# The delta rule's decay in the copy of the values, and its state products as two of 64 rows

## The chip, the cores and the metric

The kernel runs on one core of one Trainium2 chip. The metric is the device time of one execution in microseconds; lower is better.

## What is computed

Two transformer blocks stand one behind the other. The first has a token mixer and a mixture of 32 experts; the second has two layers of attention and feed-forward on 256 + 16 tokens. The change touches only the mixer's gated delta rule, which runs for 8 heads of width 128, forward and backward over 256 context tokens and then 256 latent tokens, in chunks of 64. Cut to what matters:

```python
kd = k * jnp.exp(g[..., -1:] - g)[..., None]      # decay from each token to its chunk's end
gl = jnp.exp(g[..., -1])
...
def step(s, xs_n):                                # one chunk; s is the 128 x 128 state of a head
    u_n, w_n, attn_n, qg_n, kd_n, gl_n = xs_n
    v_new = u_n - jnp.einsum('bhck,bhkv->bhcv', w_n, s)
    o_n = jnp.einsum('bhck,bhkv->bhcv', qg_n, s) + jnp.einsum('bhij,bhjv->bhiv', attn_n, v_new)
    s = s * gl_n[..., None, None] + jnp.einsum('bhck,bhcv->bhkv', kd_n, v_new)
    return s, o_n
```

The sum over a chunk's 64 tokens of `kd` times `v_new` is the same whether the decay, one number for each token, multiplies the key or the value.

## The kernel before

One program holds the mixer and the experts' weights of the first block, and the second block behind them. In the mixer, the projections of the input by `w_in` are float32 products in three parts each (`mm3`, L164): ACT rounds a weight piece to its high part (L150), DVE takes the low part (L151), and PE runs high·high, high·low and low·high. A framework schedules each engine's instructions: it takes the program as written and reorders it by what is ready in its own reckoning, so the order on an engine isn't the order of the code. Memory and PSUM tiles come from pools with a fixed number of buffers for each tag.

The delta rule runs in an order written as a string of letters (`DELTA_ORDER`, L169): K, Q and V are the convolved projections, M and X a group's inverse matrices, H is `head_setup` for one head, S is `scan_step` for a pair of heads, and small letters are fill work, mainly projections of other parts of the mixer. There are four pairs of heads, each with two H and eight S, one after the other.

`head_setup` (L649) copies the keys to token-major form (`kt`, by `to_tok`, L647), builds the attention matrix `A2` (L666, L667) and the inverse `TT` (L677 to L688; `Dt`, `Dn`, `Z`, `E` in the trace). Then it makes two arrays of 8 steps x 128 columns, by four instructions of 64 partitions x 512 elements each (L695): `vs`, the values times beta, on DVE, and `ks`, the keys times the decay `eDL`, on POOL. `comb` (L455 on) puts forward chunk `cf` into one half of the partitions of step n and backward chunk `cb` into the other. POOL also clears `vb` (L702), a 128 x 256 tile for each of two steps in turn.

`scan_step` (L706) treats both directions of one head at once. For step n:

- `p1` (L718, L719): two products of the state `st` with the keys, 64 output rows each, in two column halves of the array, which run side by side. DVE makes `r` from it (L721).
- `vn` (L724): TT times `r`, 128 x 128.
- ACT copies `vn`'s forward rows into columns 0 to 127 of `vb` (L726) and its backward rows into columns 128 to 255 (L727); the rest of `vb` stays zero.
- in steps 4 to 7 the outputs `o1` (L731, L732), a second copy of `vn` (L734), `o2` (L736), and their sum (L737, L738).
- `pu` (L742): one product of `ks` with `vb`, 128 x 128 weights and 256 columns, which gives both directions' state update thanks to the zeros. In step 0 DVE copies it to `st` (L744), later it adds it to the decayed state, 128 columns at a time (L746, L748). Step 7 has none, so there are 56 such products.

At a pair's end DVE adds the two directions' outputs (L756). PSUM's eight banks go to `mm` (2), `sm` (2), `ch` (3, the small products above) and `pu` (1). Behind the delta rule, four heads of gated linear attention (GLA) use `pu` for two products each (L866, L870). Tiles `y` are the mixer's 12 large buffers (three for each pair: `TT`, `vs`, `ks`), of which three are alive at a time.

Behind the mixer the experts' weights are loaded by the SP queue as buffers come free and multiplied as they arrive.

Of the kernel before, what the change touches and what calls it, by code (L numbers as in the profile page):

```python
# [9 lines left out]
F32 = mybir.dt.float32  # L10
F32R = mybir.dt.float32r
I32 = mybir.dt.int32
AF = mybir.ActivationFunctionType
# [180 lines left out]
def phase1(k, A, B):  # L194
# [28 lines left out]
    def chps():  # L223
        return ps.tile([128, 128], F32, name=k.nm("ch"), tag="ch", bufs=3)
# [5 lines left out]
    def big(shape, dt=F32):  # L230

        return y8.tile([128] + shape, dt, name=k.nm("y8"), tag="y8")
# [227 lines left out]
    ceG = one.tile([128, 8, 8], F32, name="ceG")  # L460
    comb(cnbe, lambda r, d, q: nc.vector.tensor_copy(d, tv(nbe[:, :, 8 * q:8 * q + 8])[r]))
    comb(ceG, lambda r, d, q: nc.vector.tensor_copy(d, tv(eG[:, :, 8 * q:8 * q + 8])[r]))

# [80 lines left out]
    def fill_mod(j):  # L544
        mp = ps.tile([128, 512], F32, name=k.nm("ch"), tag="ch", bufs=3)
# [104 lines left out]
    def head_setup(h, TT, vs, ks):  # L650
# [48 lines left out]
        comb(ks, scaled(nc.gpsimd, kt, eDL))  # L699
        st = wd.tile([128, 256], F32, name=k.nm("st"), tag="st", bufs=2)  # L700
        vb = wd.tile([128, 2, 256], F32, name=k.nm("vb"), tag="vb", bufs=2)
        nc.gpsimd.memset(vb, 0.0)  # L702
        os_ = wd.tile([128, 4, 128], F32, name=k.nm("os"), tag="os", bufs=2)
        return A2, TT, vs, ks, st, vb, os_

    def scan_step(p, n):  # L706
# [5 lines left out]
        for h in hs:  # L712
            A2, TT, vs, ks, st, vb, os_ = sets[h]
# [11 lines left out]
            vq = vb[:, u]  # L725
            nc.scalar.copy(vq[rf, 0:128], vn[rf])  # L726
            nc.scalar.copy(vq[rb, 128:256], vn[rb])  # L727
# [12 lines left out]
            if n < 7:  # L740
                pu = ps.tile([128, 256], F32, name=k.nm("pu"), tag="pu", bufs=1)
                nc.tensor.matmul(pu, ks[:, n, :], vq, start=True, stop=True)  # L742
                if n == 0:
                    nc.vector.tensor_copy(st, pu)  # L744
                else:
                    nc.vector.scalar_tensor_tensor(st[:, 0:128], st[:, 0:128], gl[:, h, cf:cf + 1],  # L746
                                                   pu[:, 0:128], op0=ALU.mult, op1=ALU.add)
                    nc.vector.scalar_tensor_tensor(st[:, 128:256], st[:, 128:256], gl[:, 8 + h, cb:cb + 1],  # L748
                                                   pu[:, 128:256], op0=ALU.mult, op1=ALU.add)
# [11 lines left out]
    for c in DELTA_ORDER:  # L761
# [25 lines left out]
        elif c == "H":  # L787
            if i % 2 == 0:
                trio = [big([2, 8, 128]) for _ in range(3)]
            sets[i] = head_setup(i, *(x[:, i % 2] for x in trio))  # L790
# [769 lines left out]
T2 = 272  # L1560
# [539 lines left out]
```

## Time and profile before

| | us |
|---|---|
| median of 3 runs (lowest, highest) | 2473.36 (2466.64, 2479.65) |
| the profiled execution, its own time | 2471.81 |
| span of its instructions | 2470.0 |
| PE busy in the span | 2284.5 (92%) |
| DVE busy | 1243.4 (50%) |
| ACT busy | 925.4 (37%) |
| POOL busy | 151.0 (6%) |

The delta rule's scans and setups lie between 165 and 480 us of the span, GLA and the merge behind them to about 690, the experts to about 1700, and the second block behind those. The 1.8 us between the span and the execution's own time lie before and after the recorded instructions. An engine's share over the whole span mixes these stages, so the rows are read by stretches: in each one, which engine is busy for nearly all of it, and what the others wait for. In a timeline, a row is one instruction or a run of like ones (x count); the time in brackets is idle time of that engine just ahead of it, with the instruction that ended it. A float32 product shows as two passes (x2) on PE.

### The profile page before, as it was taken

How to read it: one execution, taken by the hardware profiler on the slowest of the kernel's cores; microseconds unless marked ns; L12 is line 12 of the kernel's file. 1: busy time of each engine (PE TensorE's matmuls, PEld its weight loads, DVE VectorE, ACT ScalarE, POOL GpSimd, SP SyncE). 2: the span in 40 equal slices, each digit the busy share in tenths (PEclk: the TensorE clock that was granted, in tenths of full speed). 3: DMA queues.
4: the chain of work that ended last, by engine and by line, in shares of the span. 5: the costliest groups of instructions: out<-in, count | busy, mean ns of one | idle time of the engine just before them, and what ended most of it. 6: DMA issues, size and time to landing. Idle time of an engine off the chain costs nothing.

```text
span 2470.0 us, 36281 instructions
## 1 busy us (share of the span) xinstructions
PE 2284.5 (92%) x14402; PEld 1546.0 (63%) x14403; DVE 1243.4 (50%) x2676; ACT 925.4 (37%) x1956; POOL 151.0 (6%) x186
## 2 busy tenths in 40 slices
PE   6789978999989999999899999998999999999998
PEld 3466646889983333333334333334877999887998
DVE  4898897587561111112211111114867556866655
ACT  4556546577441101010101010103475545465544
POOL 0122012000010000000000000000011001011001
PEclk8889988999999999999999999999999999999999
DMA  8522431134898999999999999996524555534563
GB/s 286 142 77 52 120 120 35 45 94 121 254 329 325 416 416 416 416 416 416 388 415 415 416 415 416 416 416 237 157 84 151 179 175 160 153 103 140 188 187 104
DMA packets 290347, 605.87 MB, mean 245 GB/s; under 512 B 26038, under 2 KB 218681, under 8 KB 254332
## 3 DMA queue, kind: packets, MB, share of 16 engines
q1 hardware_dynamic: 283236, 595.24, 65.8%
q10 hardware_dynamic: 6280, 7.80, 1.2%
q8 instruction: 115, 1.88, 0.3%
q14 instruction: 60, 0.49, 0.1%
q0 software_dynamic: 656, 0.46, 0.1%
HBM read 602.30 MB, written 1.15 MB: 244 GB/s over the span
## 4 chain that ended last, share of the span: by engine, by line
PE 35%; DMA 9%; DVE 4%; issue 2%; ACT 1%; POOL 0%; ACTq 0%; SPq 0%; DVEq 0%; POOLq 0%
PE qm L164 23%; DMA w<-in_w_gu_dram 6%; PE yd L1374 2%; DMA w<-in_w_down_dram 2%; PE gt L1358 2%; PE lt L1358 2%; PE qm L1811 1%; DVE wl L151 1%; PE tr L1343 1%; DVE u L1617 0%; PE tr L1287 0%; PE qp L1878 0%; ACT wh L150 0%; PE lt L1363 0%; PE qp L1823 0%
## 5 line engine op out<-in xcount | busy, mean ns | idle before, releaser
L150 ACT CAST wh<-w 128x1024 fp32r<-128x1024 f32 (+2 forms) x318 | 318.4, 1002 | 284.7 <-PE qm L164 203.0
L151 DVE TENSOR_TENSOR wl<-w,wh 128x1024 fp32r<-128x1024 f32 (+2 forms) x318 | 371.1, 1168 | 40.5 <-ACT wh L150 38.9
L1253 ACT ACTIVATE sg<-g 128x1024 f32<-128x1024 f32 x16 | 16.9, 1057 | 727.3 <-DVE g L1251 682.7
L164 PE MATMUL qm<-uh,wh 128*128 128x272 f32 (+2 forms) x1008 | 261.4, 293 | 0.5 <-ACT wh L150 0.3
L164 PE MATMUL qm<-ul,wh 128*128 128x272 f32 (+2 forms) x1008 | 258.0, 289 | 1.0 <-DVE ul L151 1.0
L1251 DVE TENSOR_SCALAR g<-gt 128x1024 f32<-128x1024 f32 x16 | 19.6, 1225 | 469.4 <-PE gt L1363 413.9
L1374 PE MATMUL yd<-w,aT 128*64 128x512 f32 x1024 | 228.4, 600 | 0.2 <-ACT aT L1265 0.2
L164 PEld LDWEIGHTS qm<-uh,wh 128*128 128x128 f32 (+1 forms) x1008 | 188.9, 188 | 10.2 <-issue 5.8
L164 PEld LDWEIGHTS qm<-ul,wh 128*128 128x128 f32 (+1 forms) x1008 | 189.7, 188 | 2.9 <-DVE ul L151 1.4
L1358 PE MATMUL lt<-w,resB 128*64 128x512 f32 x512 | 189.5, 594 | 0.6 <-DVE act L1252 0.6
L1358 PE MATMUL lt<-w,xg 128*64 128x512 f32 x512 | 188.4, 597 | 0.0
L1358 PE MATMUL gt<-w,resB 128*64 128x512 f32 x512 | 183.0, 600 | 5.3 <-DMA w<-in_w_gu_dram 5.3
L1358 PE MATMUL gt<-w,xg 128*64 128x512 f32 x512 | 177.3, 602 | 8.9 <-DMA w<-in_w_gu_dram 8.8
L1374 PEld LDWEIGHTS yd<-w,aT 128*64 128x64 f32 x1024 | 72.9, 138 | 143.3 <-issue 140.3
L164 PE MATMUL qm<-uh,wl 128*128 128x272 f32 (+2 forms) x1008 | 145.6, 286 | 0.0
L1273 DVE TENSOR_TENSOR ys<-yd,g2r 128x512 f32<-128x512 f32 x32 | 20.6, 686 | 248.1 <-PE yd L1374 231.4
L164 PE MATMUL mm<-hTh,wh 128*128 128x256 f32 (+1 forms) x384 | 130.6, 360 | 8.2 <-ACT wh L150 4.1
L164 PEld LDWEIGHTS qm<-uh,wl 128*128 128x128 f32 (+1 forms) x1008 | 132.7, 188 | 0.5 <-issue 0.4
L164 PE MATMUL qm<-fl,wh 128*128 128x272 f32 (+1 forms) x512 | 128.5, 286 | 0.0
L164 PE MATMUL qm<-fh,wh 128*128 128x272 f32 (+1 forms) x512 | 127.3, 286 | 0.0
L164 PE MATMUL mm<-hTl,wh 128*128 128x256 f32 (+1 forms) x384 | 126.1, 348 | 0.0
L1358 PEld LDWEIGHTS lt<-w,xg 128*64 128x64 f32 x512 | 60.4, 138 | 71.4 <-issue 69.3
(586 smaller groups left out, 4349.8 us busy)
## 6 DMA issues: line engine op xcount, KB each, us to landing
w<-in_w_gu_dram SPq DMA_DIRECT2D x256, 1024.0 KB
w<-in_w_down_dram SPq DMA_DIRECT2D x128, 1024.0 KB
w<-in_w_ff_dram SPq DMA_DIRECT2D x64, 1024.0 KB
w<-in_w_in_dram SPq DMA_DIRECT2D x72, 512.0 KB
w<-in_w_in_dram SPq DMA_DIRECT2D x30, 1024.0 KB
y<-in_w_mod_dram SPq DMA_DIRECT2D x19, 1024.0 KB
w<-in_w_out_dram SPq DMA_DIRECT2D x24, 512.0 KB
w<-in_w_mod_dram SPq DMA_DIRECT2D x5, 1024.0 KB
```

The source lines that it names most:

```text
L150: k.nc.scalar.copy(hi, x)
L151: k.nc.vector.tensor_sub(lo, x, hi.bitcast(F32))
L164: mm = nc.tensor.matmul(out, l, r, start=start and n == 1, stop=stop and n == 3 * len(terms))
L1251: nc.vector.tensor_scalar(g, gt, 7.0, LOW / 1.702, op0=ALU.min, op1=ALU.max)
L1253: nc.scalar.activation(sg, g, AF.Exp, scale=-1.702)
L1273: nc.vector.tensor_mul(ys[:, js], yd[:, js], g2r[:, js])
L1343: nc.tensor.matmul(o, hx[:, t, f * 128:(f + 1) * 128], S[t].rearrange("p e s -> p (e s)"), start=(t == 0 and i == 0), stop=(t == 1 and i = ...
L1358: nc.tensor.matmul(quarter(j)[64 * i:64 * i + 64], xg[:, kk, c0:c0 + CAP], w[i][:, j * 512:(j + 1) * 512], start=(kk == 0), stop=False)
L1374: nc.tensor.matmul(yd[64 * i:64 * i + 64, j * 512:(j + 1) * 512], aT[:, 2 * f2 + f, 64 * i:64 * i + 64], w[i][:, f, j * 512:(j + 1) * 512] ...
L1811: nc.tensor.matmul(o[r, f:], v[:n, j, r], keys(ts[i], j, n)[:, f - KQ[j]:], start=(j == 0), stop=(j == 2))
```

## The change

- The decay moves from the keys to the values. `ks` and its four POOL instructions for each head are gone, and so are `vb`'s clearing on POOL and one of three large `y` buffers for each pair. `head_setup` hands on the plain `kt` instead.
- A small table `ceDL`, the decay in step order, is built once by four small DVE copies like those of `ceG` (L462).
- One ACT instruction copies the whole `vn` (128 x 128) to `vb`, scaled by `ceDL`'s column of that step and head, in place of two copies of 64 rows. `vb` is half as wide. Step 7 has no copy any more.
- The state product is two products of 64 rows each, forward on one half of the array's rows and backward on the other: weights are 64 rows x 128 columns of `kt`, and 128 columns of values go through. Each writes a `ch` tile of its own. Step 0 copies them to `st` by two instructions of 128 columns.
- The bank of `pu` goes to `ch`, which has four buffers now. GLA's two products go to `ch` too, and its `G` moves from the tag `kt` to `vt`.

```diff
-        return ps.tile([128, 128], F32, name=k.nm("ch"), tag="ch", bufs=3)
+        return ps.tile([128, 128], F32, name=k.nm("ch"), tag="ch", bufs=4)
...
+    ceDL = one.tile([128, 8, 8], F32, name="ceDL")
...
+    comb(ceDL, lambda r, d, q: nc.vector.tensor_copy(d, tv(eDL[:, :, 8 * q:8 * q + 8])[r]))
...
         comb(vs, scaled(nc.vector, vts[hh], Bt))
-        comb(ks, scaled(nc.gpsimd, kt, eDL))
         st = wd.tile([128, 256], F32, name=k.nm("st"), tag="st", bufs=2)
-        vb = wd.tile([128, 2, 256], F32, name=k.nm("vb"), tag="vb", bufs=2)
-        nc.gpsimd.memset(vb, 0.0)
+        vb = wd.tile([128, 2, 128], F32, name=k.nm("vb"), tag="vb", bufs=2)
...
-            vq = vb[:, u]
-            nc.scalar.copy(vq[rf, 0:128], vn[rf])
-            nc.scalar.copy(vq[rb, 128:256], vn[rb])
+            if n < 7:
+                vq = vb[:, u]
+                nc.scalar.activation(vq, vn, AF.Copy, scale=ceDL[:, n, h:h + 1])
...
             if n < 7:
-                pu = ps.tile([128, 256], F32, name=k.nm("pu"), tag="pu", bufs=1)
-                nc.tensor.matmul(pu, ks[:, n, :], vq, start=True, stop=True)
-                if n == 0:
-                    nc.vector.tensor_copy(st, pu)
-                else:
-                    nc.vector.scalar_tensor_tensor(st[:, 0:128], st[:, 0:128], gl[:, h, cf:cf + 1],
-                                                   pu[:, 0:128], op0=ALU.mult, op1=ALU.add)
-                    nc.vector.scalar_tensor_tensor(st[:, 128:256], st[:, 128:256], gl[:, 8 + h, cb:cb + 1],
-                                                   pu[:, 128:256], op0=ALU.mult, op1=ALU.add)
+
+                pu = chps(), chps()
+                nc.tensor.matmul(pu[0], kt[rf, cf // 2, :], vq[rf], start=True, stop=True)
+                nc.tensor.matmul(pu[1], kt[rb, cb // 2, :], vq[rb], start=True, stop=True)
+                for d, c in enumerate((cf, cb)):
+                    sd = st[:, 128 * d:128 * d + 128]
+                    if n == 0:
+                        nc.vector.tensor_copy(sd, pu[d])
+                    else:
+                        nc.vector.scalar_tensor_tensor(sd, sd, gl[:, 8 * d + h, c:c + 1], pu[d], op0=ALU.mult, op1=ALU.add)
...
-                trio = [big([2, 8, 128]) for _ in range(3)]
-            sets[i] = head_setup(i, *(x[:, i % 2] for x in trio))
+                duo = [big([2, 8, 128]) for _ in range(2)]
+            sets[i] = head_setup(i, *(x[:, i % 2] for x in duo))
...
-        G = T2("G", "kt")
+        G = T2("G", "vt")
...
-        p0 = ps.tile([128, 256], F32, name=k.nm("pu"), tag="pu", bufs=1)
+        p0 = ps.tile([128, 256], F32, name=k.nm("pu"), tag="ch", bufs=4)
```

With the code, the scheduler's order changes through the mixer. PE in the fourth pair's early steps, before (L164 are projections that fill the time, named `tm`):

```order
L724 MATMUL ch_4138<-r_4136,y_675_3939 128x128
L164 MATMUL tm_4436<-wh_4464,hTh 128x256
L164 MATMUL tm_4436<-wh_4464,hTl 128x256
L718 MATMUL ch_4146<-st_4020,kT_2658 64x128
L164 MATMUL tm_4436<-wh_4464,hTh 128x256
L742 MATMUL pu_4142<-vb_4103,y_677_3941 128x256
L719 MATMUL ch_4146<-st_4020,kT_2658 64x128
L164 MATMUL tm_4436<-wh_4464,hTl 128x256
L164 MATMUL tm_4436<-wh_4464,hTh 128x256
```

After, the same place; L743 and L744 are the two new products, other lines of the scan keep their numbers:

```order
L724 MATMUL ch_4182<-r_4180,y_714_3947 128x128
L164 MATMUL tm_4562<-wh_4532,hTl 128x256
L164 MATMUL tm_4562<-wh_4532,hTh 128x256
L164 MATMUL tm_4562<-wh_4532,hTl 128x256
L164 MATMUL tm_4562<-wh_4532,hTh 128x256
L743 MATMUL ch_4185<-vb_4024,kt_3954 128x128
L744 MATMUL ch_4186<-vb_4024,kt_3954 128x128
L718 MATMUL ch_4191<-st_4100,kT_2726 64x128
L719 MATMUL ch_4191<-st_4100,kT_2726 64x128
L164 MATMUL tm_4562<-wh_4532,hTl 128x256
L164 MATMUL tm_4562<-wl_4533,hTh 128x256 x4
```

Before, the two halves of `p1` (L718, L719) of one head stand apart, with fill work and the other head's state product between them; in the whole scan 11 of the 56 pairs are parted so. After, all 56 pairs stand whole, nearly always right behind the two state products of the other head.

POOL from the fourth pair's setup on, before (L669 and L655 clear TT and A2; `y` from `kt` is `ks`):

```order
L669 MEMSET y_675_3939 128x1024 x2
L702 MEMSET vb_4021 128x512
L655 MEMSET A_680_3949 128x512
L702 MEMSET vb_4103 128x512
L655 MEMSET A_692_4031 128x512
L695 TENSOR_TENSOR y_677_3941<-kt_3947,tok 64x4x128
L695 TENSOR_TENSOR y_677_3941<-kt_3947,tok 64x2x2x128
L695 TENSOR_TENSOR y_677_3941<-kt_3947,tok 64x4x128
L695 TENSOR_TENSOR y_677_3941<-kt_3947,tok 64x2x2x128
```

After (the lines moved by two: L671, L657 for L669, L655; L489 clears a convolution's border, L860 is GLA's):

```order
L671 MEMSET y_714_3947 128x1024 x2
L489 MEMSET pad_3823 128x654
L489 MEMSET pad_3918 128x654
L657 MEMSET A_718_3956 128x512
L657 MEMSET A_730_4033 128x512
L860 MEMSET AT_4697 128x256
```

The eight multiplications of each pair and the clearing of `vb` are gone from POOL, 40 rows in all, and nothing else takes their place there.

On DVE the instructions stay the same but for the four copies of `ceDL` and one more copy at step 0 of each head. On SP, whose loads are ordered by free buffers, a few loads of `w_in` and `w_mod` change places. The order of the experts' work and of the second block is the same in both.

## Rows read from the trace of the kernel before

**Rows 1.** stretches: window, its length; busy us (instructions) PE, PEld, DVE, ACT, POOL; PEclk, DMA, GB/s
```profile
230.00:250.00 20.00, 18.27 (x132) 12.70 (x131) 17.61 (x32) 12.82 (x33) 10.01 (x10) 0.83 0.51 78
...
292.00:360.00 68.00, 51.59 (x430) 32.18 (x429) 63.92 (x148) 28.27 (x55) 12.13 (x15) 0.87 0.47 160
...
418.00:436.00 18.00, 12.58 (x156) 10.51 (x157) 14.73 (x22) 9.43 (x38) 11.11 (x10) 0.62 0.00 1
436.00:480.00 44.00, 44.00 (x312) 34.42 (x313) 21.70 (x60) 19.01 (x60) 0.63 (x2) 1.00 0.18 48
...
800.00:1600.00 800.00, 750.55 (x3244) 296.58 (x3242) 142.28 (x211) 73.92 (x106) 1.09 (x2) 0.99 1.01 414
```

**Rows 2.** timeline of POOL, 405 to 440: start us, us, engine, line, op, tiles, count [idle before]
```profile
420.22 10.25 POOL L695 TENSOR_TENSOR y<-kt,tok 64x512 f32<-64x512 f32 x8
```

**Rows 3.** timeline of DVE, 420 to 433
```profile
421.74 2.45 DVE L756 TENSOR_TENSOR resB<-os 64x256 f32<-64x256 f32 x2
424.20 4.35 DVE L695 TENSOR_TENSOR y<-vt,tok 64x512 f32<-64x512 f32 x3
...
429.62 3.31 DVE L695 TENSOR_TENSOR y<-vt,tok 64x512 f32<-64x512 f32 x4
```

**Rows 4.** timeline of PE, 417 to 433.5
```profile
428.70 0.77 PE L724 MATMUL ch<-y,y 128*128 128x128 f32 x2 [3.57 <-DVE y L695]
```

**Rows 5.** line L695's instructions: duration ns min/median/max, first and last start
```profile
L695 DVE TENSOR_TENSOR y<-vt,tok x32: 674/689/1536, 156.4 to 432.2; 64x512 f32<-64x512 f32 x32
L695 POOL TENSOR_TENSOR y<-kt,tok x32: 1040/1201/1500, 165.9 to 429.4; 64x512 f32<-64x512 f32 x32
```

**Rows 6.** the same view of line L756
```profile
L756 DVE TENSOR_TENSOR resB<-os x16: 406/422/1258, 228.8 to 477.9; 64x256 f32<-64x256 f32 x16
```

**Rows 7.** timeline of DVE, 227 to 247
```profile
233.95 2.84 DVE L695 TENSOR_TENSOR y<-vt,tok 64x512 f32<-64x512 f32 x3
...
237.85 4.26 DVE L695 TENSOR_TENSOR y<-vt,tok 64x512 f32<-64x512 f32 x4
```

**Rows 8.** timeline of DVE, 340 to 348
```profile
343.07 1.21 DVE L631 TENSOR_TENSOR tmp<-Ms,Ts 128x207 f32<-128x207 f32 x1
...
344.40 1.02 DVE L633 TENSOR_TENSOR Ts<-Ts,tmp 128x207 f32<-128x207 f32 x1
...
346.90 0.36 DVE L633 TENSOR_TENSOR Ts<-Ts,tmp 128x192 f32<-128x192 f32 x1
```

**Rows 9.** timeline of all engines, 445.1 to 448.4
```profile
445.53 0.59 PE L742 MATMUL pu<-vb,y 128*128 128x256 f32 x2
...
446.06 0.43 PE L719 MATMUL ch<-st,kT 128*64 128x128 f32 x2
...
446.42 0.39 PE L164 MATMUL tm<-wh,hTh 128*128 128x256 f32 x1
...
446.64 0.28 PE L164 MATMUL tm<-wh,hTl 128*128 128x256 f32 x1
...
446.76 0.29 PE L164 MATMUL tm<-wh,hTh 128*128 128x256 f32 x1
...
446.95 1.22 DVE L151 TENSOR_TENSOR wl<-w,wh 128x1024 fp32r<-128x1024 f32 x1
...
447.48 0.39 PE L724 MATMUL ch<-r,y 128*128 128x128 f32 x2
...
447.79 0.32 PE L718 MATMUL ch<-st,kT 128*64 128x128 f32 x1
...
447.95 0.26 ACT L726 COPY vb<-ch 64x128 f32<-64x128 f32 x1 [1.37 <-PE ch L724]
...
448.16 0.50 PE L164 MATMUL tm<-wl,hTh 128*128 128x256 f32 x2
```

**Rows 10.** ACT's groups, 100 to 480: line, op, shapes, count, busy us, mean ns, idle before
```profile
L727 ACT COPY vb<-ch 64x128 f32<-64x128 f32 x64 | 16.7, 260 | 0.8
```

**Rows 11.** DVE's groups, 100 to 480, the same columns
```profile
L744 DVE COPY st<-pu 128x256 f32<-128x256 f32 x8 | 3.4, 424 | 1.8 <-PE pu L742 1.7
```

More of the change, by code (lines that the diff above doesn't have):

```diff
@@ L544, in fill_mod @@
     def fill_mod(j):
-        mp = ps.tile([128, 512], F32, name=k.nm("ch"), tag="ch", bufs=3)
+        mp = ps.tile([128, 512], F32, name=k.nm("ch"), tag="ch", bufs=4)
         for kk in range(8):
@@ L648, in to_tok, with head_setup @@
         return vt
-    def head_setup(h, TT, vs, ks):
+    def head_setup(h, TT, vs):
         hh, h, (M, EA, Dn, Dt) = h, h % 4, groups[h // 4]
@@ L698, in head_setup @@
         comb(vs, scaled(nc.vector, vts[hh], Bt))
-        comb(ks, scaled(nc.gpsimd, kt, eDL))
         st = wd.tile([128, 256], F32, name=k.nm("st"), tag="st", bufs=2)
-        vb = wd.tile([128, 2, 256], F32, name=k.nm("vb"), tag="vb", bufs=2)
-        nc.gpsimd.memset(vb, 0.0)
+        vb = wd.tile([128, 2, 128], F32, name=k.nm("vb"), tag="vb", bufs=2)
         os_ = wd.tile([128, 4, 128], F32, name=k.nm("os"), tag="os", bufs=2)
-        return A2, TT, vs, ks, st, vb, os_
+        return A2, TT, vs, kt, st, vb, os_
     def scan_step(p, n):
@@ L712, in scan_step @@
         for h in hs:
-            A2, TT, vs, ks, st, vb, os_ = sets[h]
+            A2, TT, vs, kt, st, vb, os_ = sets[h]
             if n == 0:
@@ L805, in gla_gates @@
         kT, qT = gk[h], gq[h]
-        pz = ps.tile([128, 512], F32, name=k.nm("ch"), tag="ch", bufs=3)
+        pz = ps.tile([128, 512], F32, name=k.nm("ch"), tag="ch", bufs=4)
         nc.tensor.matmul(pz, gw[32 * d:32 * d + 16, h * 128:(h + 1) * 128], lr[32 * d:32 * d + 16, :], start=True, stop=True)
-        T2 = lambda nm, tag, b=2: (wd if tag == "kt" else wk).tile([128, 512], F32, name=k.nm(nm), tag=tag, bufs=b)
+        T2 = lambda nm, tag, b=2: (wd if tag == "vt" else wk).tile([128, 512], F32, name=k.nm(nm), tag=tag, bufs=b)
         z, l = T2("z", "acc"), T2("l", "e", 3)
@@ L869, in gla_gates @@
         nc.scalar.copy(ss_[:, 0, :], p0)
-        p1 = ps.tile([128, 256], F32, name=k.nm("pu"), tag="pu", bufs=1)
+        p1 = ps.tile([128, 256], F32, name=k.nm("pu"), tag="ch", bufs=4)
         nc.tensor.matmul(p1, kdt[:, 2, :], gv[h][:, 2 + fi, :], start=True, stop=True)
@@ L1040, in ev_out @@
         return fn
-    pl = [ps.tile([128, 32], F32, name=k.nm("pl"), tag="ch", bufs=3) for _ in range(2)]
+    pl = [ps.tile([128, 32], F32, name=k.nm("pl"), tag="ch", bufs=4) for _ in range(2)]
     def logits(cc):
```

## The prediction

> **What bounds the kernel now.** I read the table of stretches first [rows 1], since the shares over the whole span mix stages. While the experts run (800 to 1600), the DMA engines are busy throughout (1.01 of the window): that stage has a length of its own, and what the mixer ahead of it gains or loses shifts it by as much. So the change is worth what it moves in 165 to 480, one for one. There the limit changes from place to place. In the fourth pair's scan (436 to 480) PE is busy 44.00 of 44 us at full clock: only PE time counts. In the setups between scans PE is not full: 12.58 of 18 us at clock 0.62 in 418 to 436, 18.27 of 20 at 0.83 in 230 to 250, 51.59 of 68 at 0.87 in 292 to 360, where DVE has 63.92. These are the stretches in which POOL works (11.11 of 18 and 10.01 of 20 us). So I then read DVE and POOL there, and PE's own timeline in the scan.
>
> **POOL's products slow DVE.** L695 on DVE takes 689 ns in the median, but 1536 at worst, while the same shape on POOL takes 1201 [rows 5]. POOL's eight for the fourth pair fill 420.22 to 430.5 without a gap [rows 2], and just there three DVE ones take 4.35 us and four take 3.31, and two of L756 take 2.45 [rows 3], against 0.422 each undisturbed [rows 6]. Excess: 4.35 − 3 × 0.689 = 2.28, 3.31 − 4 × 0.689 = 0.55, 2.45 − 0.84 = 1.61, in sum 4.4. PE waits for exactly this: 3.57 us before L724, until DVE's L695 [rows 4]. After, POOL has nothing to do there. I take −6 for the place: the 4.4, and 1.6 for the clock, granted at half its speed (1.2 of 2.4 GHz) for most of the 18 us, after PE had idled; it should come back sooner. Ends: −3.6 (that wait alone) and −8.
> In the second pair the same products make three L695 take 2.84 and four take 4.26 [rows 7], excess 0.77 + 1.50 = 2.3; PE idles 1.7 of the 20 us there and is at 0.83 clock [rows 1], for which I add 1.2, so −3.5 (−1.7 to −4.2). Pair one, with as many POOL products, I price alike, a little less: −3 (0 to −4).
> For the third pair they run beside the inverse of the next group, a chain of small DVE instructions: L631 takes 1.21 and L633 1.02, and the like a little later 0.36 [rows 8], excess 0.85 + 0.66; I add 1 for the same slowing of their neighbours. DVE is the limit in that stretch, so −2.5 (0 to −3).
> Sum of this part **−15** (−5 to −19).
>
> **The state products.** Before, one keeps PE for 0.43 us: L742's first pass starts at 445.53 and the next product, L719, at 446.06, of which 0.10 go to a change of mode [rows 9]; that is 0.215 for a pass of 256 columns, 0.11 for 128. After, four passes of 128 columns and 64 rows, two on each half of the rows. No row of the mixer has that form; the nearest is L718 with L719, two halves of columns that run side by side. The whole pair, from the end of the product ahead of it (447.48 + 2 × 0.11 = 447.70) to the next fill (448.16), takes 0.46, of which 0.09 ahead (447.70 to 447.79) and as much behind are spent on getting into the other mode. Since in the new order the pair P stands right behind the state products, the step between them is shared. I take 0.42 for the two state products: 0.09 to get in, about 0.22 for the passes when the halves overlap, 0.11 for a weight load that no work hides. That is 56 × (0.42 − 0.43), about **−0.8**. Bounds: −4 if it is 0.36, as cheap as the pair without its exit; +11 if the two halves don't overlap (0.63 each, 56 × 0.2).
>
> Rows 9 show what a change of mode costs, 0.09 us each way. The Trainium skill says so as a rule (TensorEngine Tiling (Array Packing), Key Properties: a change of tiling mode, not merely of tile, drains TensorE), and it speaks against this change, which adds one more mode to each step; the trace agrees, and with the rule the state product would cost 0.1 more than before where the passes save nothing, +6 in all.
>
> **The parted pairs.** In before's order 11 of the 56 pairs P are parted. A half alone costs as much as a whole pair: from 445.96 to the next fill at 446.42 it is 0.46, and that fill is 0.22 from the next one (446.42 to 446.64) where 0.12 is usual (446.64 to 446.76) [rows 9], so 0.56 in sum. After, none is parted: 11 × 0.56 = **−6.2** (−5 to −6.5), PE time in stretches where PE is full.
>
> **What is added.** Step 0 has two copies to `st` in place of one of 424 ns [rows 11], eight times; on the way to the next step it is about +0.1 each, **+1** (0 to +2). The four copies of `ceDL` are 64 x 32 each, smaller than that, early in the mixer: **+0.7** at most, likely under DMA waits. ACT makes one copy of 128 rows in place of two of 64 rows, 260 ns each [rows 10]; with the same 128 columns I take it to last as long as one of them: each state product may start some 0.26 earlier, worth little where fills stand in between: **−1** (0 to −3).
>
> **The order.** After, the schedule is stricter: L724, four fills, the two state products and P at once, fills again. L724's result takes 0.47 to reach ACT (447.48 to 447.95) and the copy 0.26 more [rows 9]; PE gets through L724 and four fills in 0.23 + 4 × 0.12 = 0.71. So PE comes 0.02 to 0.1 early in each of 56 head-steps, and what DVE has in front of `st` and `r` adds to it now and then. The four `ch` buffers are also all used in one late step (vn, o1, o2, and two for the state), and two of GLA's products wait for them. I take **+5** (0 to +10).
>
> Sum: −15 − 0.8 − 6.2 + 1 + 0.7 − 1 + 5 = −16.3. Against the profiled execution's own 2471.81 that is 2455.5; the median of the runs is 1.5 above it, so **2457**.
>
> **Rivals.**
> - *The halves don't run side by side* (the change doesn't do what it says): two products of 64 rows cost 0.42 + 2 × 0.11, about 0.63, for each step instead of 0.43, +11, and the gains at the setups stay: 2457 + 11 = 2468. For it: both halves read `vb` and write PSUM at once, and no row shows that form; against it: L718 and L719, halves of the array too, take 0.46 with all their entering and leaving, which four passes one behind the other of 0.11 would fill by themselves.
> - *DVE or PE's place in the order takes the gain back.* POOL's products are gone, yet the setup's DVE chain keeps its length in PE's waits because new order puts other DVE work there, or fills run out at the ends of pairs two and three: half of the −15 is lost and +5 becomes +9: −16.3 + 7.5 + 4 = −5, 2468 again; range 2462 to 2474.
> - *Better*: all the DVE excess passes to the end (−19) and the state products cost 0.36 (−4): −19 − 4 − 6.2 + 1 + 2 = −26, 2447; up to 2440 where the order costs nothing.
> - *Slower*: the alternation itself. With P right behind the state products, and T's `r` behind both `st` updates on DVE, each head-step is one chain; a 1.22 us L151 [rows 9] in front of the updates then stops PE, since the fills behind it are few. To cancel 16.3 it has to cost 0.29 on top in each of the 56 head-steps, or one whole L151 in 13 of them. If it meets 24, 24 × 1.22 = +29, 2457 + 29 = 2486. For it: PE has no idle time in that stretch now, with more room between products. Against it: fills are as many as before, and the scheduler parts most L151 from the chain.
>
> **Chances.** The forecast, 2445 to 2461, has 0.53; better 0.08; the halves one behind the other 0.12; gain mostly taken back 0.17; slower 0.10, of which 0.07 lies beyond half a per cent. Half a per cent, 12.4 us, is about what a measurement of this kernel can tell from no change. The rivals at 2468 count as within it. Faster (below 2461): 0.61; same: 0.32; slower (above 2486): 0.07. The range leaves out the slower case and the best part of the better one: 2441 to 2474.
>
> **What would show it.** In the changed kernel's trace: no POOL L695; DVE's L695 all near 0.69 us, PE's wait before the fourth pair's first L724 near zero and the clock of that stretch well above 0.62 (if not, the −15 is wrong). The two state products starting 0.01 to 0.05 apart, and from the end of the fill ahead of them to P about 0.42 (0.63 would show the serial rival). No P alone. In the scans PE still near full; a wait before P or L724 on DVE of over 0.2 us in most steps would show the slower rival. The expert stage should keep its length and begin earlier by the gain; if it doesn't, a transfer sets its start, and the prediction is wrong at its first step.

## The result and the profile after

The changed kernel takes 2489.35 us (2488.23 to 2493.58, 5 runs) against 2473.36 (2466.64 to 2479.65, 5 runs) of the kernel before: 1.0065 times, with a 95% interval of 1.0046 to 1.0084. It is slower by some 16 us, where 2457 was forecast. The profiled execution took 2488.23 with a span of 2486.5.

Stretches, with the columns of [rows 1]. The bounds are the first and last L724 of a pair's scan, GLA from behind the last scan to its last state product, and from there to the first product behind the mixer, all to within 2 us (the changed kernel's bounds lie 0.9 us behind these products). First the kernel before: between the scans of pairs 1 and 2, 2 and 3, the third scan, between 3 and 4, GLA, and the mixer's rest.

```profile
228.50:236.90 8.40, 6.71 (x82) 4.70 (x80) 8.19 (x14) 7.15 (x23) 7.84 (x8) 1.00 0.00 0
292.60:367.30 74.70, 57.83 (x516) 36.66 (x514) 69.43 (x153) 33.78 (x77) 12.13 (x15) 0.89 0.47 156
367.30:417.80 50.50, 48.53 (x389) 37.56 (x385) 35.53 (x89) 32.12 (x93) 7.91 (x9) 0.97 0.19 52
417.80:428.70 10.90, 5.93 (x100) 4.47 (x100) 10.16 (x14) 7.83 (x30) 9.33 (x9) 0.66 0.01 2
474.70:596.60 121.90, 119.06 (x835) 105.09 (x834) 98.79 (x250) 87.45 (x214) 2.19 (x7) 1.00 0.32 88
596.60:660.00 63.40, 60.59 (x482) 58.87 (x480) 40.18 (x81) 41.55 (x101) 2.34 (x1) 0.97 0.72 213
```

The same six of the changed kernel:

```profile
227.50:234.00 6.50, 6.50 (x92) 4.82 (x92) 5.71 (x13) 3.66 (x9) 0.53 (x1) 1.00 0.49 164
290.30:354.00 63.70, 50.07 (x408) 34.31 (x408) 60.15 (x145) 31.96 (x70) 8.88 (x12) 0.85 0.48 163
354.00:409.90 55.90, 53.20 (x470) 41.64 (x470) 31.83 (x90) 31.98 (x89) 1.17 (x2) 0.81 0.11 30
409.90:417.10 7.20, 4.21 (x65) 3.33 (x63) 6.22 (x16) 2.99 (x13) 0.53 (x1) 0.71 0.00 0
466.00:623.00 157.00, 134.21 (x861) 114.79 (x860) 102.15 (x255) 91.59 (x221) 2.01 (x7) 0.92 0.27 76
623.00:676.70 53.70, 51.16 (x410) 49.10 (x408) 35.52 (x71) 35.77 (x88) 2.37 (x1) 1.00 0.71 211
```

The setups between scans are shorter: 8.4 to 6.5, 74.7 to 63.7, 10.9 to 7.2 us, in sum 16.6. They also hold less: counted by their start, 547 PE instructions lie in the three where before has 690, since work of the next setups moved into the scans. The first GLA product starts 10.4 us earlier (476.6 to 466.2), with 33 more of the projections' fill products (L164) already done, some 4 us. Then GLA takes 157.0 us where it took 121.9, with PE busy for 134.2 of them and a clock of 0.92 instead of 1.00: of the 35 us more, PE idles 20 (22.8 against 2.8) and is busy 15 longer, at that clock and with 38 more fill products, some 4 us. The rest of the mixer gives some 10 of that back: part of its fill work has been done by then. Counted between the starts of products: −10.4 to GLA's first, +37.2 in GLA (118.0 to 155.2), −11.0 to the first product behind the mixer (660.0 to 675.8 in the span), +0.7 in all that follows; in sum +16.5. So the loss is in one stage, and it is one that the change touches by the tags of three tiles only.

DVE's products of the values, in the view of [rows 5], and the fourth pair's setup on DVE, which answers to [rows 3]:

```profile
L697 DVE TENSOR_TENSOR y<-vt,tok x32: 673/684/691, 155.0 to 418.2; 64x512 f32<-64x512 f32 x32
```

```profile
411.55 0.85 DVE L757 TENSOR_TENSOR resB<-os 64x256 f32<-64x256 f32 x2
...
412.64 2.59 DVE L697 TENSOR_TENSOR y<-vt,tok 64x512 f32<-64x512 f32 x4
...
416.29 2.59 DVE L697 TENSOR_TENSOR y<-vt,tok 64x512 f32<-64x512 f32 x4
```

All 32 take 673 to 691 ns, where the median was 689 and the worst 1536; four of them take 2.59 us, and two of L757 (before: L756) 0.85 instead of 2.45. POOL has no instruction there.

Why GLA is longer: one direction of a head is a gate product (L807 before, L808 after), a long chain on DVE and ACT, attention products on two lines (L862 and L863 before, L863 and L864 after), three transposes, and state products on two lines (L868, L871 before; L869, L872 after). What PE waits for in GLA, by line, releaser, total us, times, longest; first before, then after:

```profile
PE ch L862 <- DVE qk L835: 2.8, 6, 0.6
```

```profile
PE ch L863 <- DVE qk L836: 15.2, 7, 5.1
```

PE's timeline at one such place, before:

```profile
486.73 0.71 PE L862 MATMUL ch<-qk 128*128 128x128 f32 x4 [0.42 <-DVE qk L835]
...
487.75 1.12 PE L807 MATMUL ch<-lr,gw 16*128 16x512 f32 x2
...
490.65 1.04 PE L868 MATMUL pu<-gv,kdt 128*128 128x256 f32 x4
...
492.23 0.65 PE L871 MATMUL pu<-gv,kdt 128*128 128x256 f32 x2
```

Attention at 486.73, the next direction's gate right behind it at 487.75, and only then, among fills, this direction's state products at 490.65 and 492.23. After, a like place:

```profile
519.06 0.71 PE L863 MATMUL ch<-qk 128*128 128x128 f32 x4 [0.15 <-DVE qk L836]
...
522.13 2.03 PE L869 MATMUL pu<-gv,kdt 128*128 128x256 f32 x4 [0.57 <-ACT kdt L858]
523.96 1.06 PE L872 MATMUL pu<-gv,kdt 128*128 128x256 f32 x2
524.95 1.44 PE L808 MATMUL ch<-lr,gw 16*128 16x512 f32 x2
...
533.45 0.77 PE L863 MATMUL ch<-qk 128*128 128x128 f32 x2 [5.14 <-DVE qk L836]
```

The gate (524.95) comes behind both state products now, 5.9 us after the attention product (519.06) instead of 1.0; over the seven handovers from one direction to the next it is 3.6 to 24.9 us instead of 1.0 to 1.5. The chain from the gate to the next attention product takes 8 to 11 us in both, where PE waits for it; started late, it outlasts the fills, and PE waits 5.14 us before L863. In all seven handovers of the changed kernel the gate stands behind L872; before, it stood ahead of L868. The granted clock falls in stretches with such waits, to 0.74 and 0.83 in these two of 20 us:

```profile
520.00:540.00 20.00, 13.43 (x44) 9.08 (x43) 13.05 (x39) 9.46 (x31) 0.31 (x1) 0.74 0.18 53
...
560.00:580.00 20.00, 15.06 (x91) 13.32 (x92) 9.89 (x25) 8.22 (x19) 0.53 (x2) 0.83 0.08 21
```

### The profile page after: what moved, and what is told of

Read it like the earlier page. It is cut to its first block, busy times and chain, and to the rows that moved or that the text cites. A ratio compares the mean times of both kernels' runs of the same rounds, so it can differ in the third digit from the quotient of the medians.

```text
span 2486.5 us, 36348 instructions
## 1 busy us (share of the span) xinstructions
PE 2288.4 (92%) x14514; PEld 1547.0 (62%) x14515; DVE 1226.2 (49%) x2688; ACT 914.3 (37%) x1884; POOL 109.7 (4%) x146
## 3 DMA queue, kind: packets, MB, share of 16 engines
q1 hardware_dynamic: 283236, 595.24, 65.6%
## 5 line engine op out<-in xcount | busy, mean ns | idle before, releaser
L151 DVE TENSOR_TENSOR wl<-w,wh 128x1024 fp32r<-128x1024 f32 (+2 forms) x318 | 373.3, 1175 | 53.8 <-ACT wh L150 52.1
L164 PE MATMUL qm<-uh,wh 128*128 128x272 f32 (+2 forms) x1008 | 261.0, 293 | 0.5 <-ACT wh L150 0.3
L164 PE MATMUL qm<-ul,wh 128*128 128x272 f32 (+2 forms) x1008 | 257.5, 289 | 0.9 <-DVE ul L151 0.9
L164 PEld LDWEIGHTS qm<-uh,wh 128*128 128x128 f32 (+1 forms) x1008 | 188.7, 188 | 10.2 <-issue 5.8
L164 PEld LDWEIGHTS qm<-ul,wh 128*128 128x128 f32 (+1 forms) x1008 | 189.4, 188 | 2.8 <-DVE ul L151 1.3
L164 PE MATMUL qm<-uh,wl 128*128 128x272 f32 (+2 forms) x1008 | 144.7, 285 | 0.0
L164 PE MATMUL mm<-hTh,wh 128*128 128x256 f32 (+1 forms) x384 | 127.1, 351 | 6.6 <-ACT wh L150 4.1
L164 PEld LDWEIGHTS qm<-uh,wl 128*128 128x128 f32 (+1 forms) x1008 | 131.9, 187 | 0.5 <-issue 0.4
L164 PE MATMUL qm<-fl,wh 128*128 128x272 f32 (+1 forms) x512 | 128.5, 286 | 0.0
L164 PE MATMUL qm<-fh,wh 128*128 128x272 f32 (+1 forms) x512 | 127.3, 286 | 0.0
L164 PE MATMUL mm<-hTl,wh 128*128 128x256 f32 (+1 forms) x384 | 123.7, 341 | 0.0
```

What stands on the lines that cost most here:

```text
L151: k.nc.vector.tensor_sub(lo, x, hi.bitcast(F32))
L164: mm = nc.tensor.matmul(out, l, r, start=start and n == 1, stop=stop and n == 3 * len(terms))
```

## The experiments

In this table "delta" is the time from the first L724 to the last, "scans" what the four scans take of it, and GLA is counted from its first gate to its last state product, all in the profiled execution; the time is the median, the ratio is to runs of the kernel before on the same chip. A profiled execution can lie up to 10 us from its kernel's median (e5_products_gla_sm 2477.76, e7_full_rows 2480.03, e8_idle_pool 2485.14). The scans don't hold the same work in all kernels, since each schedule parts setups and fill differently: 1404 PE instructions start in them before, 1690 in the changed kernel, e3, e9 and e10, 1694 in e2, 1615 in e1, 1496 in e6, 1848 in e7, 1556 in e11. Their lengths compare like with like only where these counts agree.

| kernel | us | ratio (95%) | delta | scans | GLA |
|---|---|---|---|---|---|
| before | 2473.36 | | 303.5 | 209.4 | 118.0 |
| changed | 2489.35 | 1.0065 (1.0046 to 1.0084) | 292.8 | 215.4 | 155.2 |
| e1_before_merge | 2518.17 | 1.0188 (1.0171 to 1.0205) | 325.1 | 239.7 | 153.4 |
| e2_own_bank | 2475.16 | 1.0011 (0.9996 to 1.0026) | 301.7 | 222.2 | 120.2 |
| e3_gla_sm | 2462.49 | 0.9954 (0.9941 to 0.9967) | 291.3 | 213.6 | 119.5 |
| e4_products_alone | 2493.41 | 1.0076 (1.0063 to 1.0089) | 321.4 | 217.0 | 118.3 |
| e5_products_gla_sm | 2468.72 | 0.9974 (0.9965 to 0.9983) | 303.7 | 209.1 | 121.0 |
| e6_decay_alone | 2459.73 | 0.9944 (0.9928 to 0.9961) | 286.2 | 199.6 | 121.5 |
| e7_full_rows | 2489.97 | 1.0065 (1.0050 to 1.0080) | 313.3 | 236.9 | 117.0 |
| e8_idle_pool | 2492.50 | 1.0076 (1.0062 to 1.0090) | 310.1 | 212.7 | 131.2 |
| e9_late_states | 2488.43 | 1.0064 (1.0048 to 1.0081) | 292.8 | 215.9 | 152.7 |
| e10_gates_first | 2464.82 | 0.9967 (0.9951 to 0.9982) | 290.5 | 212.3 | 120.0 |
| e11_both_heads | 2465.19 | 0.9976 (0.9959 to 0.9992) | 294.0 | 202.5 | 120.3 |

**Where the loss comes from.** The theory is that the tag `ch` is one ring of buffers whose tiles are handed out in the order of the code. GLA's state products take two of them, so the next direction's gate, which takes a `ch` tile too, can't come before them. First the merge of the banks alone, without the rest of the change:

```diff
-        return ps.tile([128, 128], F32, name=k.nm("ch"), tag="ch", bufs=3)
+        return ps.tile([128, 128], F32, name=k.nm("ch"), tag="ch", bufs=4)
...
-                pu = ps.tile([128, 256], F32, name=k.nm("pu"), tag="pu", bufs=1)
+                pu = ps.tile([128, 256], F32, name=k.nm("pu"), tag="ch", bufs=4)
...
-        p0 = ps.tile([128, 256], F32, name=k.nm("pu"), tag="pu", bufs=1)
+        p0 = ps.tile([128, 256], F32, name=k.nm("pu"), tag="ch", bufs=4)
...
```

> The kernel before with one thing of the change alone: the bank of pu goes to ch (four buffers), so that the old state product and GLA's two products take their tiles from ch in turn. Delta rule, POOL's products and the 128x256 state product stay as before. Ring theory (the loss lies in GLA, where each direction's gate tile now has to come behind the two state products of the direction ahead in the same ring of buffers): GLA, from its first gate product to its last state product, lasts about 153 us as in the changed kernel instead of 116, and the whole is 20 to 35 us slower than before, 2493 to 2508. Rival (the loss comes from the delta rule's new products and the order of its fills): within 6 us of before, 2467 to 2480.

It took 2518.17, 44 us more than before, slower than the range given. GLA is 153.4, with the same wait (PE's waits, as above):

```profile
PE ch L862 <- DVE qk L835: 17.1, 8, 5.1
```

The rest is in the delta rule, 325.1 us instead of 303.5. There each P (the pair L718, L719) stands behind the other head's state product now, where before it stood ahead of it in 25 places: the old state product in the ring does to P what GLA's do to the gate. That this order alone costs that much isn't shown, since e3_gla_sm below has it too. For the loss in GLA the delta rule's new products are not needed, nor is the move of `G` to `vt`, which this run leaves out.

The other way round, the change with the merge undone, in two ways:

```diff
-        return ps.tile([128, 128], F32, name=k.nm("ch"), tag="ch", bufs=4)
+        return ps.tile([128, 128], F32, name=k.nm("ch"), tag="ch", bufs=3)
...
-                pu = chps(), chps()
+                pu = chps(), ps.tile([128, 128], F32, name=k.nm("pu"), tag="pu", bufs=1)
...
-        p0 = ps.tile([128, 256], F32, name=k.nm("pu"), tag="ch", bufs=4)
+        p0 = ps.tile([128, 256], F32, name=k.nm("pu"), tag="pu", bufs=1)
...
```

> The changed kernel with the bank of pu given back: ch has three buffers, one of the two new state products writes a ch tile and the other a tile in pu's bank, and GLA's two products use pu's bank as before. Ring theory: GLA lasts 116 us (within 6) again, the gain of the delta rule (10 to 13 us) reaches the end, 2456 to 2466 us, 7 to 17 faster than before. Rival (the delta rule uses up the fill work that GLA needs, or the second block's clock is lower): GLA stays above 140 us, 2480 or more.

GLA is back at 120.2 as the theory has it, but the time is 2475.16, above the range: with three `ch` buffers and one state tile still among them, the scans take 222.2, where the next run, with as much work in them, has 213.6. The bank is worth something to the delta rule.

```diff
-        p0 = ps.tile([128, 256], F32, name=k.nm("pu"), tag="ch", bufs=4)
+        p0 = ps.tile([128, 256], F32, name=k.nm("pu"), tag="sm", bufs=2)
...
```

> The changed kernel with only GLA's two state products moved, from ch to the tag sm (two buffers, shared with the transposes of GLA's keys); the delta rule keeps four ch buffers. Ring theory: the next direction's gate no longer waits for these products, GLA lasts 116 to 125 us and the whole is 2456 to 2472. Rival (fill work used up by the delta rule, or ch's fourth buffer itself changes GLA): 2480 or more.

2462.49 us and 119.5 for GLA: moving two tiles of GLA, and nothing in the delta rule, gives 27 us back, both within the ranges given, and the change is then faster than before. `G` keeps the tag `vt` here and in e2_own_bank, so that move isn't the loss.

Order or crowding? Five tiles for each direction in four buffers could hold PE back in any order. Two more runs keep the tiles and buffers and change the order of GLA's code alone:

```diff
+        yield
...
-            two[i] = [gla_gates(i, d) for d in range(2)]
+            gates = [gla_gates(i, d) for d in range(2)]
+            for x in gates:
+                next(x)
+            two[i] = [next(x) for x in gates]
```

> The changed kernel with GLA's code in another order and nothing else: a head's two directions both run down to their attention products before either takes its tiles for the state products, all still from the four ch buffers. If the ring hands out its tiles in the order of the code, and this order is what holds the second direction's gate back, half of the gates (those of each head's second direction) come early again: GLA lasts 128 to 145 us instead of 155, and the whole is 2465 to 2480. If it is the crowding of four buffers by five tiles for each direction, whatever their order: GLA stays at 150 us or more, 2485 or more.

A miss: GLA 152.7 and 2488.43 us, which is in the range given for crowding. The second gate of each head does come earlier (11.8, 11.5, 10.8 and 11.4 us behind the first, instead of 13.9, 16.3, 15.1 and 15.0), but the next head's gate now stands behind four state products, and those intervals grow from 28.5, 16.7 and 33.1 to 33.3, 21.3 and 37.9. So the order decides where a gate stands, but this run didn't tell the two theories apart. The next one takes every gate ahead, across heads:

```diff
+        yield
...
+    gates = {0: gla_gates(0, 0)}
+    next(gates[0])
...
+            f, b = gates.pop(i), gla_gates(i, 1)
+            next(f)
+            next(b)
+            two[i] = [next(f)]
+            next(b)
+            if i < 3:
+                gates[i + 1] = gla_gates(i + 1, 0)
+                next(gates[i + 1])
+            two[i].append(next(b))
```

> The changed kernel with GLA's code in a third order and nothing else: each direction's gate takes its ch tile before the direction ahead takes its two for the state products, across heads too. The same tiles, the same four buffers, five tiles for each direction. If the ring hands out its tiles in the order of the code and this is what held the gates back: each gate stands right behind the attention products of the direction ahead, GLA lasts 117 to 124 us as in e3_gla_sm (119.5) instead of 155, the whole 2456 to 2468. If it is the crowding of the four buffers: GLA at 145 us or more, 2480 or more.

GLA is 120.0 and the time 2464.82, with all tiles still in the four buffers. PE's timeline at its first handover (L808 the gate, L871 and L874 the state products), and its wait before the attention products:

```profile
477.32 1.12 PE L808 MATMUL ch<-lr,gw 16*128 16x512 f32 x2
478.37 1.13 PE L871 MATMUL pu<-gv,kdt 128*128 128x256 f32 x4
479.34 0.60 PE L874 MATMUL pu<-gv,kdt 128*128 128x256 f32 x2
```

```profile
PE ch L864 <- DVE qk L837: 4.9, 5, 2.5
```

Order it is, not crowding: in all seven handovers the gate stands ahead of the state products again, and 25 us of the whole come back by the order of the code alone. The same rule in the scan:

```diff
-        for h in hs:
+        def one_head(h):
...
+            if n < 4:
+                yield
...
+        heads = [one_head(h) for h in hs]
+        for x in heads * 2 if n < 4 else heads:
+            next(x)
```

> e10_gates_first with the scan's first four steps written so that both heads of a pair take their tiles for p1 and vn before either takes its two for the state products; the last four steps as they were. If the same rule of the ring is what puts each P behind the other head's state products and lengthens the scans, the four scans (54.4, 56.3, 55.9 and 48.9 us in the changed kernel, 215 in sum) are shorter by 4 to 12 us in sum, 2448 to 2460. If PE's order there is set by fill work: within 3 us of e10_gates_first.

The scans get shorter by 9.8 us (212.3 to 202.5), as expected, but the time doesn't (2465.19): the stretch between the second and the third scan takes 76.6 us instead of 63.6. It holds 511 PE instructions instead of 408, and the second scan 310 instead of 404: work of the next setup that used to lie in the second scan now lies behind it. So the shorter scans are at least in part work moved out of them, and the run doesn't show that the ring's order makes them longer. What decides where that work lies was not tried.

**What the change's own parts are worth.** With the decay left on the keys (POOL works as before), only the products change:

```diff
         comb(vs, scaled(nc.vector, vts[hh], Bt))
+        comb(ks, scaled(nc.gpsimd, kt, eDL))
...
-                nc.scalar.activation(vq, vn, AF.Copy, scale=ceDL[:, n, h:h + 1])
+                nc.scalar.copy(vq, vn)
...
-                nc.tensor.matmul(pu[0], kt[rf, cf // 2, :], vq[rf], start=True, stop=True)
+                nc.tensor.matmul(pu[0], ks[rf, n, :], vq[rf], start=True, stop=True)
...
```

On the banks of e2_own_bank:

> The variant with pu's bank given back (e2_own_bank), but the decay stays on the keys: POOL makes ks as before, the two products of 64 rows take their weights from it, and ACT copies vn unscaled in one instruction. So it is the new products without the removal of POOL's work. If POOL's multiplications slow DVE on the path, as the prediction has it (-15), it is 10 to 17 us slower than e2_own_bank, 2468 to 2480, and DVE's products of the values show a mean near 980 ns again. Rival (POOL's work is off the path and the gain of the delta rule is that of the products): within 4 us of e2_own_bank.

And the same on those of e3_gla_sm:

> e3_gla_sm (four ch buffers for the delta rule, GLA's two state products in the tag sm), but the decay stays on the keys: POOL makes ks, the two products of 64 rows take their weights from it, and ACT copies vn in one unscaled instruction. Against before it shows the products of 64 rows with four buffers alone, against e3_gla_sm the removal of POOL's work alone. Theory (the whole gain is POOL's, the new products are worth nothing in either direction once they have buffers): 2472 to 2484, 10 to 20 slower than e3_gla_sm, and the stretch between the second and the third pair's scan (74.7 us before, 63.7 in the changed kernel) is 72 us or more. Rival (the gain is that of the products and whole pairs P): 2458 to 2468.

POOL's work, with the third large buffer that it needs, costs 18 us on e2_own_bank's banks (2493.41 against 2475.16), a little more than the 10 to 17 expected, and 6 on e3_gla_sm's (2468.72 against 2462.49), less than the 10 to 20 expected and just above the rival's range. The sign is as expected in both, and so is the stretch between the second and the third scan in the latter (75.7). The products alone are worth −5.6 us with four buffers (e5 against before) and cost 19 with three (e4). Then the decay alone, with no tile of 64 rows and the banks as before (ACT scales its two copies of 64 rows):

```diff
-                nc.tensor.matmul(pu, ks[:, n, :], vq, start=True, stop=True)
+                nc.tensor.matmul(pu[:, 0:128], kt[:, cf // 2, :], vq[:, 0:128], start=True, stop=True)
+                nc.tensor.matmul(pu[:, 128:256], kt[:, cb // 2, :], vq[:, 128:256], start=True, stop=True)
```

> The kernel before with the decay moved to the values alone: no ks on POOL, two ACT copies of 64 rows scaled by the table, and the state product as two products of all 128 rows of kt (weights of the forward and of the backward chunk), 128 columns each, into one tile of pu's own bank; zeros in vb mask the other direction as before. No tile of 64 rows, no added change of mode, ch with three buffers, GLA as before. Theory (the gain is POOL's removal): 2454 to 2464, GLA 116 to 122 us, the stretch between the second and the third scan 62 to 67 us. Rival (halves of rows are needed for the gain): 2468 or more.

2459.73, the lowest of all, though its interval overlaps that of e3_gla_sm: half of the change, without its new form of product. Time and GLA (121.5) are as expected; the stretch between the second and the third scan isn't, 71.8 us where 62 to 67 were given. With POOL's multiplications put back there, and the third large buffer that they write, their result unread:

```diff
         comb(vs, scaled(nc.vector, vts[hh], Bt))
+        comb(ks, scaled(nc.gpsimd, kt, eDL))
...
-                duo = [big([2, 8, 128]) for _ in range(2)]
+                trio = [big([2, 8, 128]) for _ in range(3)]
...
```

> e6_decay_alone with POOL's 32 multiplications put back, their result read by nobody: keys times the decay, into a large buffer as before. PE's and ACT's work is that of e6_decay_alone; only POOL's traffic beside DVE, and the buffer, are added. Contention theory (POOL's multiplications slow DVE where DVE is waited for): 6 to 16 us slower than e6_decay_alone, 2466 to 2476, DVE's products of the values above 900 ns in the mean, the stretch between the second and third scan 70 us or more (71.8 in e6_decay_alone, 74.7 before), that between the third and fourth 9 us or more (7.5 and 10.9). Rival (the gain of e6_decay_alone is that of its shorter chain in the scans): 2458 to 2463.

It takes 2492.50, more than expected. DVE's products of the values, first without and then with POOL's (columns of [rows 11]), and the three stretches between scans in the same order:

```profile
L697 DVE TENSOR_TENSOR y<-vt,tok 64x512 f32<-64x512 f32 x32 | 21.2, 683 | 0.3
```

```profile
L697 DVE TENSOR_TENSOR y<-vt,tok 64x512 f32<-64x512 f32 x32 | 30.9, 991 | 0.4
```

```profile
226.50:233.70 7.20, 7.20 (x97) 5.29 (x96) 6.31 (x16) 4.75 (x14) 0.53 (x1) 1.00 0.43 148
282.30:354.10 71.80, 50.92 (x489) 32.08 (x489) 66.87 (x151) 33.66 (x72) 8.07 (x11) 0.83 0.49 162
406.30:413.80 7.50, 7.05 (x119) 5.75 (x119) 6.83 (x17) 4.59 (x15) 0.53 (x1) 1.00 0.01 2
```

```profile
224.20:234.90 10.70, 7.61 (x97) 5.36 (x96) 9.67 (x13) 3.84 (x10) 9.18 (x8) 1.00 0.00 0
292.00:368.00 76.00, 51.33 (x501) 33.82 (x499) 71.63 (x160) 37.31 (x78) 12.64 (x16) 0.82 0.39 134
422.60:433.30 10.70, 6.70 (x108) 5.31 (x106) 9.75 (x14) 4.68 (x17) 9.22 (x8) 0.85 0.01 2
```

POOL busy for 9.18 of 10.70 us and DVE's products at 991 ns instead of 683: the three stretches grow by 3.5, 4.2 and 3.2, 10.9 in sum, with as much work in them (699 PE instructions against 698). The two profiled executions are 23 us apart (2485.14 and 2462.15): the scans take 13 more and GLA 10 more, and some 11 are given back ahead of the first scan and behind GLA. In GLA one handover has the gate behind the state products, which e6_decay_alone has nowhere. How much of the scans' 13 is contention and how much order isn't shown. The Trainium skill states the contention (SBUF — State Buffer, Who interferes with whom: a DVE instruction with two SBUF inputs contends with a GpSimd instruction that reads SBUF); these rows agree and give its size here, 45% on DVE's mean.

Last, e6_decay_alone with the banks of e3_gla_sm:

```diff
-                pu = ps.tile([128, 256], F32, name=k.nm("pu"), tag="pu", bufs=1)
+                pu = ps.tile([128, 256], F32, name=k.nm("pu"), tag="ch", bufs=4)
...
-        p0 = ps.tile([128, 256], F32, name=k.nm("pu"), tag="pu", bufs=1)
+        p0 = ps.tile([128, 256], F32, name=k.nm("pu"), tag="sm", bufs=2)
```

> e6_decay_alone with the banks of e3_gla_sm: the state product's one tile comes from ch (four buffers), GLA's two from sm. So a state product takes one tile of the ring where e3_gla_sm takes two, and has no change of mode. If the ring's places are what makes the scans of the changed kernel longer (54.4, 56.3, 55.9, 48.9 us against 57.3, 55.7, 50.5, 46.0 before), its scans are shorter than those of e3_gla_sm by 1 us or more each, and it takes 2450 to 2460; if it is fill work and order, 2460 to 2470.

2489.97, a miss: 30 us above the one range given and 20 above the other. The third and fourth scans of e6_decay_alone, then of e7_full_rows:

```profile
354.10:406.30 52.20, 52.20 (x428) 41.37 (x427) 37.46 (x98) 38.91 (x104) 2.86 (x5) 1.00 0.18 52
413.80:460.60 46.80, 46.36 (x359) 38.55 (x358) 20.96 (x60) 21.24 (x63) 0.31 (x1) 0.93 0.12 35
```

```profile
356.10:419.60 63.50, 56.56 (x468) 44.30 (x466) 33.47 (x91) 39.04 (x106) 2.21 (x4) 0.87 0.12 34
427.00:486.50 59.50, 59.02 (x433) 48.52 (x434) 27.51 (x70) 27.54 (x79) 0.31 (x1) 0.97 0.19 55
```

Nothing differs but the banks, and from the first L724 to the last it is 27 us longer (313.3 against 286.2); the scans alone are longer by 37, but part of that is work moved into them. In PE's order each P stands behind the other head's state product again, as in e1_before_merge, where e6_decay_alone has it ahead in 26 places. But e3_gla_sm has the same order and scans of 213.6 us with 1690 PE instructions, so the order alone doesn't explain the loss. Unlike there, two scaled copies (361 and 362 ns) stand one behind the other ahead of each state product, and 12 of the 56 pairs P are parted, where e3_gla_sm has none. No run tells these apart: the cause of this loss stays open.

## Why the prediction was wrong

- **The order**, +5 (0 to +10), is the step that failed, and with it the premise that the change is worth what it moves in 165 to 480: GLA lies behind that. "Two of GLA's products wait for them" names the place, but it was priced among delays of 0.1 us. The two products don't wait; they make another product wait, the next direction's gate, which stood ahead of them in before's order. It measured +37 in GLA, 27 us of the whole with GLA's two tiles moved (2489.35 against 2462.49) and 25 with only the order of the code changed (2464.82). The trace of before showed the gate 1.0 us behind the attention product and 2.9 ahead of the state products, and the new order has it behind both, but the place lies behind the stretch that was priced.
- **The slower rival** had the kind of mechanism (a chain made strict by the order) and nearly its time, 2486, but put it in the scan and had L151 decide it. It had 0.10, and that its time comes near is chance.
- **POOL's work**, −15 (−5 to −19): the three stretches lost 16.6 us in sum, but that the size fits is luck. By place it is −1.9, −11.0 and −3.7 where −3.5, −2.5 and −6 were put, and the −3 ahead of the first scan didn't come: it starts at 172.3 instead of 171.2. Much of the −11.0 is work that moved into the scan ahead (408 PE instructions instead of 513). e1_before_merge, with POOL's work as before, also has 403 there and takes 65.6 us instead of 74.7. Where the three stretches hold as much as before, POOL's removal takes 7.5 us off them (94.0 in before, 86.5 in e6_decay_alone), and putting the multiplications back adds 10.9. PE's wait of 3.57 us ahead of the fourth pair's first L724 is gone, as said; the granted clock of the 18 us behind the third scan rose only from 0.62 to 0.70, and the third scan ran at 0.81 instead of 0.97.
- **The state products**, 0.42 (−0.8 in sum): right. From the changed kernel, a place where PE waits for the copy and one where it doesn't:

```profile
438.74 0.37 ACT L727 ACTIVATE vb<-ch,ceDL 128x128 f32<-128x128 f32 x1 [2.13 <-PE ch L724]
...
439.16 0.37 PE L743 MATMUL ch<-vb,kt 64*128 64x128 f32 x1
...
439.17 0.37 PE L744 MATMUL ch<-vb,kt 64*128 64x128 f32 x1
...
439.58 0.32 PE L718 MATMUL ch<-st,kT 128*64 128x128 f32 x1
...
456.71 0.38 PE L736 MATMUL ch<-vn,A 128*128 128x128 f32 x2
457.03 0.37 PE L743 MATMUL ch<-vb,kt 64*128 64x128 f32 x1
...
457.45 0.32 PE L718 MATMUL ch<-st,kT 128*64 128x128 f32 x1
```

  L743 and L744 start 0.01 apart, so the halves run side by side, and P follows 0.42 behind their start (439.16 to 439.58). These 0.42 end with the step into P's mode. At the second place the step into their own mode shows too: L736's two passes of 0.11 end at 456.93, L743 starts at 457.03, P at 457.45. From the end of the product ahead to P that is 0.52, and it was 0.53 before (445.53 to 446.06 in [rows 9]), so the price holds; the sign given for it, 0.42 over that distance, left out one of the two steps. The rival with serial halves is out.
- **ACT's copy**, −1, had the wrong sign. A scaled copy of 128 rows takes 367 ns, not 260: first the changed kernel's, then the unscaled one of e5_products_gla_sm (columns of [rows 10]):

```profile
L727 ACT ACTIVATE vb<-ch,ceDL 128x128 f32<-128x128 f32 x56 | 20.5, 367 | 38.8 <-PE ch L724 38.5
```

```profile
L726 ACT COPY vb<-ch 128x128 f32<-128x128 f32 x56 | 14.9, 266 | 48.8 <-PE ch L723 48.4
```

  In the timeline above, the copy ends at 439.11 and PE has waited 0.25 for it. What PE waited for before the first state product (us, times), first after, then before:

```profile
  ACT vb L727: 9.4, 27
```

```profile
  ACT vb L727: 4.8, 10
```

  So 9.4 us in 27 places instead of 4.8 in 10: some +4.6. With the unscaled copy, e5_products_gla_sm has 4.2 in 12 places.
- **The parted pairs**: none is parted after, as said. Their −6.2 can't be found: the scans are 6 us longer, not shorter (209.4 to 215.4), but hold 1690 PE instructions instead of 1404. e6_decay_alone parts 8 pairs and is as fast as e3_gla_sm, which parts none. What a parted pair costs by itself was not tried.
- **The first step** held: the experts' stage starts later by what GLA lost and keeps its length (from its first product to its last 956.5 us before, 956.7 after).

With GLA's two tiles moved, the change comes to 2462.49: the other terms summed to −21 without the order's +5, and the measured gain is 12 (against 2474.28 on its chip).

## What to carry to other kernels

With a framework like this one, a change of PSUM banks is a change of order: tiles of one tag are handed out in the order of the code, so a short product that shares a ring with a late one can't run ahead of it. Before merging two tags, list every user of both and ask which of them runs ahead of the other today, also far from the edit. And look at the new order of the busy engine in every stage that holds an edited line, not only in the stage that the edit is meant for. Last, a stage that got shorter may only hold less: count its instructions before calling the difference a gain.

## What the hardware showed that was not expected

- ACT's copy with a scale read from memory for each partition takes 367 ns (ACTIVATE in the trace) where the plain one (COPY) takes 266 at the same 128 x 128 elements: 101 ns more. The Trainium skill has it (ScalarE: Activation LUTs, What ACT_TABLE_LOAD costs: each pointer operand of that kind adds about 93 ns), and the traces agree within 8.
- Two products of 64 rows on opposite halves start 0.01 us apart and take 0.42 us together with one step into another mode (0.52 with two), no more than one product of 128 rows and 256 columns (0.43, and 0.53 with one). But two products of all 128 rows with half their inputs zero, in a bank of their own, made a kernel as fast (e6_decay_alone, 0.9944 with 0.9928 to 0.9961, against 0.9941 to 0.9967 of e3_gla_sm): the form of 64 rows was not what paid.
